# Sums of the weights for Strassen's scheme: formed in DRAM by transfers that add, in place of VectorE

## The chip, the cores and the metric

The kernel runs on one core of one Trainium2 chip. Time is device microseconds of one execution of the whole program; the lower, the better. Kernels are compared on the same chip in alternating rounds. Engines are named as the profile names them: PE is TensorE (PEld its weight loads), DVE is VectorE, ACT is ScalarE, POOL is GpSimd and SP is SyncE. ACT, POOL and SP each have a queue that issues transfers; a transfer is carried out by the core's 16 DMA engines.

## The reference

One layer of a streaming encoder on 512 tokens of 1024 channels, all in float32. What bears on the change are two of its products, the mixers' output projection and the MLP's down-projection.

```python
h = _rms_norm(x, norm_mix_pre[l])
(a_q, a_k, a_v, f_q, f_k, f_v, f_g, c_u, s_x, s_b, s_c) = jnp.split(h @ w_in[l], cuts, axis=-1)
...
proj = jnp.einsum('bsnc,ncd->bsnd', br, w_branch[l])
gates = jax.nn.sigmoid(h @ w_gate[l] + b_gate[l]).reshape(B, S, N_BRANCH, D)
mixed = jnp.sum(gates * proj, axis=2) @ w_out[l]          # (512, 1024) @ (1024, 1024)
x = x + _rms_norm(mixed, norm_mix_post[l])
...
u = _dwconv_causal(hf @ w_up[l], ffn_dw[l]) + ffn_dw_b[l]
u_g, u_v = jnp.split(u, 2, axis=-1)
yff = (jax.nn.silu(u_g) * u_v) @ w_down[l]                # (512, 2816) @ (2816, 1024)
x = x + _rms_norm(yff, norm_ffn_post[l])
```

`br` holds the four mixers' results: differential attention `ya`, forgetting attention `yf`, a convolution module and a short gated convolution. Between the mixers and the MLP stands a cross-attention into 256 memory tokens.

## The kernel before

*Products.* Each float32 product is made of three TensorE passes on a high and a low part in float32r (`mm3`): high by high, high by low, low by high. A weight tile of 128 rows by 1024 columns is loaded by SP into one of two raw tiles `wr` (L173), cast to the high part `wh` by ACT (L187), and the low part `wl` is the difference, by DVE (L188). There are four `wh` and four `wl`. `run_blocks` walks a list of jobs, most of them one such tile with 24 matmuls, and prepares three jobs ahead. A scheduler orders the instructions of each engine when the program is built; each engine then runs its own in that order.

*Background work.* The attention heads (`a_task`, `f_task`) and the convolution's normalization are generators that `bg.tick()` steps between jobs, so that their short matmuls, softmax steps and transposes lie between the jobs' long ones. POOL clears the unused halves of each head pair's q and k tile `qk` (L758), makes the reciprocal roots of the norms (`rstd_of`, L268 and L269), and for the forgetting attention the bias tiles `fbias` (L988 and L990, two buffers) that DVE adds to the scores (L994). POOL's queue also issues some loads, among them the rows `ck` (L958) that the biases are made of.

*Strassen's scheme.* The output projection (`mix_out_jobs`) and the down-projection (`down_jobs`) take the weights in pairs of 128-row blocks and each block in two halves of 512 columns. With the halves b11, b12 of a pair's first block and b21, b22 of its second, the seven products M1 to M7 need, beside the plain halves, four sums of halves. The activations' sums are made by `activation_sums`, on DVE for the output projection and on POOL for the down-projection (L564 to L567). The class `Sums` makes the weights' sums ahead of time: `load(q)` brings the two blocks of pair q to SBUF, `add(q)` makes four sums on DVE in place (L540 to L543), `store(q)` writes them to a DRAM tile, from which `load_parts` later brings what a product needs.

For w_out (four pairs, tiles `wide`, transfers on SP's queue) this is done among the first jobs of the mixers, around the gates of the short convolution; the tiles lie in the buffer that later holds the attention's v, so v is taken only in the last of its four jobs. For w_down (11 pairs, tiles `wp`, transfers on ACT's queue) it is done during the up-projection, one step a job: in the jobs of `up_jobs`, `add`, `store` and `load` take turns, each tied behind an instruction of that job by `issue_after`. The tiles `wp` share their four buffers with the tiles `dw` of the down-projection.

The order of the stages: convolution module and short convolution, their gates; v, then q and k of the differential attention with the convolution's gates between; v of the forgetting attention; its q and k with the gates of the first attention between; the last branch's gates (`last_branch_jobs`); output projection; cross-attention; up-projection; down-projection.

Of the kernel before, what the change touches and what calls it, by code (L numbers as in the profile page):

```python
# [24 lines left out]
P = 128  # L25
# [57 lines left out]
def hybrid_layer(ctx: ExitStack, tc: tile.TileContext, a: dict, out: bass.AP):  # L83
# [91 lines left out]

    def split_weights(raw, shape, low=V, order=same, shift=0):
# [10 lines left out]
        order(A.copy(hi, raw[:, :n]))  # L187
# [73 lines left out]
    def rstd_of(pool, parts, n=1):  # L261

        m = pool.tile([P, n], F32, tag="st_m", name="st_m", bufs=4)
        r = pool.tile([P, n], F32, tag="st_r", name="st_r", bufs=4)
        if len(parts) == 2:
            G.tensor_scalar(m, parts[0], parts[1], EPS, ALU.add, ALU.add)
        else:
            G.tensor_scalar(m, parts[0], EPS, None, ALU.add)  # L268
        G.tensor_tensor(r, m, nhalf[:, :n], ALU.pow)  # L269
        return r  # L270
# [254 lines left out]
    class Sums:  # L525


        def __init__(self, w, pairs, tile, queue, name):
            self.w, self.tile, self.queue, self.held = w, tile, queue, {}
            self.pairs, self.dram = pairs, dram.tile([pairs * P, 2 * D], F32, name=name)  # L530

        def load(self, q):
            if q < self.pairs:
                self.held[q] = [self.tile() for _ in range(2)]
                for i, x in enumerate(self.held[q]):
                    self.queue.dma_start(x, self.w[(2 * q + i) * P:(2 * q + i + 1) * P, :])

        def add(self, q):
            (b11, b12), (b21, b22) = ((x[:, :S], x[:, S:]) for x in self.held[q])
            V.tensor_tensor(b22, b22, b12, ALU.subtract)  # L540
            V.tensor_tensor(b12, b12, b11, ALU.subtract)
            V.tensor_tensor(b11, b22, b11, ALU.add)
            V.tensor_tensor(b21, b21, b11, ALU.subtract)  # L543

        def store(self, q):
            for i, x in enumerate(self.held.pop(q)):
                self.queue.dma_start(self.dram[q * P:(q + 1) * P, i * D:(i + 1) * D], x)

        def parts(self, phase, job, q):

            rows = [slice((2 * q + i) * P, (2 * q + i + 1) * P) for i in range(2)]
            t2, t1, n4, t3 = (self.dram[q * P:(q + 1) * P, i * S:(i + 1) * S] for i in range(4))
            return {(0, 0): (self.w[rows[0], :S], t2), (0, 1): (t1, t3), (1, 0): (self.w[rows[1], :],),
                    (1, 1): (n4,)}[phase, job]
# [194 lines left out]
    def qk_jobs(cq, ck, j, then):  # L749
# [5 lines left out]
        def body_q(hi, lo):  # L755
            qk = st["qk"] = m1p.tile([P, 6, S], F32R, tag="qk", name="qk", bufs=2)
            for c, r in enumerate(rows):
                G.memset(qk[rows[1 - c], 4 + c].bitcast(F32), 0.0)  # L758
# [192 lines left out]
    def f_task(p, qk, v):  # L951
# [10 lines left out]
        for step in range(6):  # L962
# [17 lines left out]
            if step < 4:  # L980
# [3 lines left out]
                for j in range(2):  # L984
# [5 lines left out]
                    G.affine_select(out=bias[:, w - P:w], in_=bias[:, w - P:w], pattern=[[-1, P]],  # L990
                                    compare_op=ALU.is_ge, fill=BIG, base=0, channel_multiplier=1)
# [64 lines left out]

    def kv_blocks(p):
        return qk_jobs(O_FQ, O_FK, p, lambda qk: bg.add(f_task(p, qk, vf), "f"))

    def mixer_jobs():  # L1060
# [4 lines left out]
        wide = m1p.tile([P, NT, D], F32, tag="v", name="wide")  # L1065
        free = iter([wide[:, i] for i in (0, 1, 2, 3) * 2])
        ns.out_sums = out_sums = Sums(w_out, NK // 2, lambda: next(free), SP, "out_sums")
        steps = {5: (out_sums.load, 0), 6: (out_sums.load, 1), 9: (out_sums.add, 0), 10: (out_sums.store, 0),
                 11: (out_sums.add, 1)}
        for i, job in enumerate(gate_blocks(3, "d")):  # L1070
            yield job
            if i in steps:
                yield then(lambda f=steps[i]: f[0](f[1]))
        yield then(lambda: y.pop("d"))
        vj = v_jobs(O_AV, va)
        yield then(lambda: (out_sums.store(1), out_sums.load(2), out_sums.load(3)) and None)
        for f, q in ((out_sums.add, 2), (out_sums.add, 3)):
            yield next(vj)
            yield then(lambda f=f, q=q: f(q))
            yield then(lambda q=q: out_sums.store(q))  # L1080
        yield from vj
        yield share(False)
        gc = gate_blocks(2, "c")
        for h, n in enumerate((0, 2, 4, 6)):
            yield from qk_jobs(O_AQ, O_AK, h, lambda qk, h=h: bg.add(a_task(h, qk, va), "a"))
            if n:
                yield then(lambda: bg.drain("conv"))
            for _ in range(n):
                yield next(gc)
        yield then(lambda: bg.drain("a"))  # L1090
        yield from vf_jobs(vf)
        yield from kv_blocks(0)
        ga = gate_blocks(0, "a")
        for p in range(1, 4):
            yield from kv_blocks(p)
            for _ in range(4):
# [96 lines left out]
    def last_branch_jobs():  # L1193
# [5 lines left out]
        yield from gf  # L1199
# [44 lines left out]
    def mix_out_jobs():  # L1244
# [50 lines left out]
        def middle(job):  # L1295
# [175 lines left out]
    def up_jobs():  # L1471
        st, held = {}, []

        def done(j, i, ps):
# [3 lines left out]
            st["first"] = A.activation(c[:, i], ps, AF.Identity, bias=pc("fb", ch), scale=pc("fdw2", ch)).ins  # L1478
            st["taps"] = taps(c[:, i], ps, lambda k: pc("fdw01", k * 44 + ch), 3).ins
# [252 lines left out]
```

## Time and profile before

| | |
|---|---|
| median of three runs | 1062.26 us (1062.02 to 1063.12) |
| profiled execution | 1062.36 us |
| its span, first to last instruction | 1060.5 us |
| mean granted clock of TensorE | 0.999 |
| moved by transfers in the span | 152.57 MB, 144 GB/s |

The span covers the first to the last instruction; the profiled execution's own time is 1.9 us longer. A group's row reads: line, engine, operation, output tile and inputs with shapes and count; then busy time and the mean of one in ns; then the idle time of the engine just before such instructions, with what ended it. Two rows of matmuls and the two of a weight tile's preparation:

```profile
L229 PE MATMUL ps_mm<-hth,wh 128*128 128x512 f32 (+1 forms) x616 | 231.5, 382 | 0.3 <-ACT hth L152 0.2
L229 PE MATMUL ps_mm<-htl,wh 128*128 128x512 f32 (+1 forms) x616 | 229.9, 380 | 0.0
...
L187 ACT CAST wh<-wr 128x1024 fp32r<-128x1024 f32 (+1 forms) x142 | 148.6, 1049 | 268.8 <-PE ps_mm L229 177.0
L188 DVE TENSOR_TENSOR wl<-wr,wh 128x1024 fp32r<-128x1024 f32 (+1 forms) x142 | 178.1, 1256 | 86.3 <-ACT wh L187 86.0
```

A matmul's own time here is from its start to its end through the pipeline; the next starts earlier, so rates are read from counts in a stretch of time.

### The profile page before, as it was taken

How to read it: one execution, taken by the hardware profiler on the slowest of the kernel's cores; microseconds unless marked ns; L12 is line 12 of the kernel's file. 1: busy time of each engine (PE TensorE's matmuls, PEld its weight loads, DVE VectorE, ACT ScalarE, POOL GpSimd, SP SyncE). 2: the span in 40 equal slices, each digit the busy share in tenths (PEclk: the TensorE clock that was granted, in tenths of full speed). 3: DMA queues.
4: the chain of work that ended last, by engine and by line, in shares of the span. 5: the costliest groups of instructions: out<-in, count | busy, mean ns of one | idle time of the engine just before them, and what ended most of it. 6: DMA issues, size and time to landing. Idle time of an engine off the chain costs nothing.

```text
span 1060.5 us, 14527 instructions
## 1 busy us (share of the span) xinstructions
PE 1051.5 (99%) x5363; PEld 894.0 (84%) x5363; DVE 797.1 (75%) x1261; ACT 497.6 (47%) x817; POOL 146.8 (14%) x233
## 2 busy tenths in 40 slices
PE   9999999999999999999999999999999999999997
PEld 8888888888888988888888899999888888888885
DVE  6899997567666358766575889786778787777796
ACT  5322222367565255655443565664333333445672
POOL 4000000000001015322110021031111211111001
PEclk9999999999999999999999999999999999999999
DMA  8854333322222252332344743226576776725672
GB/s 274 281 167 103 101 100 100 96 83 80 80 80 62 55 146 86 97 96 81 120 140 144 266 146 119 81 79 196 181 223 214 238 226 211 238 80 179 206 221 79
DMA packets 162107, 152.57 MB, mean 144 GB/s; under 512 B 5567, under 2 KB 135212, under 8 KB 162037
## 3 DMA queue, kind: packets, MB, share of 16 engines
q1 hardware_dynamic: 153139, 120.04, 37.7%
q10 hardware_dynamic: 6338, 23.08, 5.7%
q0 software_dynamic: 2560, 8.54, 2.7%
q8 instruction: 42, 0.69, 0.3%
q14 instruction: 28, 0.23, 0.1%
HBM read 133.79 MB, written 17.84 MB: 143 GB/s over the span
## 4 chain that ended last, share of the span: by engine, by line
PE 99%; DVE 0%; ACT 0%; issue 0%; POOLq 0%; DVEq 0%; POOL 0%; ACTq 0%
PE ps_mm L229 53%; PE ps_av L229 30%; PE ps_sc L229 7%; PE ps_tr L229 4%; PE ps_tr L233 3%; PE ps_mm L440 1%; PE ps_av L440 1%; PE ps_mm L382 0%; PE ps_sc L387 0%; DVE o L1632 0%; PE ps_tr L424 0%; DVE wr L1647 0%; DVE o L1623 0%; ACT ge L1029 0%; DVE o L1647 0%
## 5 line engine op out<-in xcount | busy, mean ns | idle before, releaser
L187 ACT CAST wh<-wr 128x1024 fp32r<-128x1024 f32 (+1 forms) x142 | 148.6, 1049 | 268.8 <-PE ps_mm L229 177.0
L188 DVE TENSOR_TENSOR wl<-wr,wh 128x1024 fp32r<-128x1024 f32 (+1 forms) x142 | 178.1, 1256 | 86.3 <-ACT wh L187 86.0
L229 PE MATMUL ps_mm<-hth,wh 128*128 128x512 f32 (+1 forms) x616 | 231.5, 382 | 0.3 <-ACT hth L152 0.2
L229 PE MATMUL ps_mm<-htl,wh 128*128 128x512 f32 (+1 forms) x616 | 229.9, 380 | 0.0
L229 PE MATMUL ps_mm<-hth,wl 128*128 128x512 f32 (+1 forms) x616 | 229.8, 379 | 0.0
L229 PEld LDWEIGHTS ps_mm<-hth,wh 128*128 128x128 f32 x616 | 114.2, 188 | 21.7 <-ACT hth L152 0.8
L229 PEld LDWEIGHTS ps_mm<-hth,wl 128*128 128x128 f32 x616 | 113.9, 188 | 21.2
L229 PEld LDWEIGHTS ps_mm<-htl,wh 128*128 128x128 f32 x616 | 114.1, 188 | 20.4 <-DVE htl L153 0.2
L229 PE MATMUL ps_av<-hth,wh 128*128 128x512 f32 (+1 forms) x328 | 122.7, 374 | 0.0
L229 PE MATMUL ps_av<-hth,wl 128*128 128x512 f32 (+1 forms) x328 | 122.5, 373 | 0.0
L229 PE MATMUL ps_av<-htl,wh 128*128 128x512 f32 (+1 forms) x328 | 122.4, 373 | 0.0
L662 DVE SCALAR_TENSOR_TENSOR y<-y,par,y 128x482 f32<-128x482 f32 (+29 forms) x120 | 82.8, 728 | 0.2
L229 PEld LDWEIGHTS ps_av<-htl,wh 128*128 128x128 f32 x328 | 61.7, 188 | 10.9
L229 PEld LDWEIGHTS ps_av<-hth,wl 128*128 128x128 f32 x328 | 61.7, 188 | 10.8
L229 PEld LDWEIGHTS ps_av<-hth,wh 128*128 128x128 f32 x328 | 61.5, 188 | 10.8
L1534 DVE TENSOR_TENSOR wl<-dw,wh 128x1024 fp32r<-128x1024 f32 x32 | 40.2, 1261 | 12.2 <-ACT wh L1533 12.1
L1533 ACT CAST wh<-dw 128x1024 fp32r<-128x1024 f32 x32 | 33.5, 1052 | 22.5 <-PE ps_tr L229 8.3
L988 POOL TENSOR_SCALAR fbias<-ck,cq 128x128 f32<-128x128 f32 (+3 forms) x32 | 27.5, 865 | 68.8 <-DVE st L994 61.9
L1482 ACT ACTIVATE th<-c 128x512 f32<-128x512 f32 x22 | 13.9, 632 | 48.5 <-DVE c L592 48.5
L152 ACT CAST pth<-ps_tr 128x512 fp32r<-128x512 f32 (+3 forms) x56 | 23.4, 448 | 21.6 <-PE ps_tr L233 21.5
L592 DVE SCALAR_TENSOR_TENSOR c<-ps_mm,par,c 128x510 f32<-128x510 f32 (+1 forms) x44 | 32.7, 744 | 0.7
L153 DVE TENSOR_TENSOR ptl<-ps_tr,pth 128x512 fp32r<-128x512 f32 (+3 forms) x56 | 27.9, 512 | 5.6 <-ACT pth L152 5.4
(466 smaller groups left out, 2099.2 us busy)
## 6 DMA issues: line engine op xcount, KB each, us to landing
wr<-in_w_up SPq DMA_DIRECT2D x44, 512.0 KB
wr<-in_w_in SPq DMA_DIRECT2D x38, 512.0 KB
wr<-in_w_gate SPq DMA_DIRECT2D x32, 512.0 KB
wp<-in_w_down ACTq DMA_DIRECT2D x22, 512.0 KB
sums<-wp ACTq DMA_DIRECT2D x22, 512.0 KB
dw<-sums SPq DMA_DIRECT2D x44, 256.0 KB
wr<-in_w_branch SPq DMA_DIRECT2D x16, 512.0 KB
wide<-in_w_out SPq DMA_DIRECT2D x12, 512.0 KB
```

Of the source, the lines that this page charges most:

```text
L152: A.copy(hi, ps)
L153: V.tensor_tensor(lo, ps, hi.bitcast(F32), ALU.subtract)
L187: order(A.copy(hi, raw[:, :n]))
L188: low.tensor_tensor(lo, raw[:, :n], hi.bitcast(F32), ALU.subtract)
L229: PE.matmul(ps, lhs, rhs, start=start, stop=stop)
L233: PE.transpose(ps, x, ident[:n, :n])
L440: keep(PE.matmul(banks[c][:, :S // 2], w[p == 1][:, k, c * P:(c + 1) * P], ht[p == 2][:, i * 4 + k, :S // 2], start=(i, p, k) == (0, 0, 0) ...
L592: ins = V.scalar_tensor_tensor(dst[:, s:], src[:, :S - s], w(k), dst[:, s:], ALU.mult, ALU.add)
L662: ins = V.scalar_tensor_tensor(dst[:, s:], src[:, :S - s], pc("conv_dw", k * 4 + j), dst[:, s:], ALU.mult, ALU.add)
L988: G.tensor_scalar(bias[:, :w], ck[j][:, :w], -1.0, cq[:, qt, head:head + 1], ALU.mult, ALU.add)
L1533: A.copy(hi, x)
L1534: V.tensor_tensor(lo, x, hi.bitcast(F32), ALU.subtract)
```

## The change

The sums of the weights are no longer made in SBUF. For each chunk of four pairs (three in w_down's last) there are four DRAM tiles p1 to p4 of 512 columns. ACT's queue copies a half into each, from DRAM to DRAM; then POOL's queue issues four transfers that add:

- p1 = b11 + b12
- p3 = b12 + b22
- p2 = b22 + p1
- p4 = b21 + p2

Before, the four were b11 + b22 - b12, b12 - b11, b22 - b12 and b21 - b11 - b22 + b12. With adding alone the second half of each block counts with the other sign, so one activation sum, the last activation sum and the combinations with M5 and M7 turn a sign; each stays one instruction of the same kind on the same operands.

The 32 steps (8 for a chunk, one chunk of w_out and three of w_down) are handed out one at a time by `sums_step`, which `paced` puts after each job from v of the differential attention to the last branch; between the steps of w_down an empty one is put, so that they come every second job. A step is tied on its engine behind the latest entry of a log: `cast_log` holds ACT's casts of weights, `pool_log` POOL's roots, clears and bias selections. Each tile of the sums is then read by `load_parts` as before.

```diff
-        def load(self, q):
-            if q < self.pairs:
-                self.held[q] = [self.tile() for _ in range(2)]
-                for i, x in enumerate(self.held[q]):
-                    self.queue.dma_start(x, self.w[(2 * q + i) * P:(2 * q + i + 1) * P, :])
-
-        def add(self, q):
-            (b11, b12), (b21, b22) = ((x[:, :S], x[:, S:]) for x in self.held[q])
-            V.tensor_tensor(b22, b22, b12, ALU.subtract)
-            V.tensor_tensor(b12, b12, b11, ALU.subtract)
-            V.tensor_tensor(b11, b22, b11, ALU.add)
-            V.tensor_tensor(b21, b21, b11, ALU.subtract)
...
+        def steps(self):
+
+            for i, sums in enumerate(self.sums):
+                n = sums[0].shape[0] // P
+                w = self.w[2 * i * self.chunk * P:][:2 * n * P]
+                b11, b12, b21, b22 = (w.rearrange("(q i p) c -> i p q c", i=2, p=P)[r][:, :, c * S:(c + 1) * S]
+                                      for r in range(2) for c in range(2))
+                p1, p2, p3, p4 = (t.rearrange("(q p) c -> p q c", p=P) for t in sums)
+
+                for dst, src in (p1, b11), (p3, b12), (p2, b22), (p4, b21):
+                    yield cast_log, lambda dst=dst, src=src: A.dma_start(dst, src)
+                for dst, src in (p1, b12), (p3, b22), (p2, p1), (p4, p2):
+                    yield pool_log, lambda dst=dst, src=src: G.dma_start(dst, src, accum_op=ALU.add)
...
-        eng.tensor_tensor(x[:, 2], x[:, 1], z[:, 1], ALU.add)
+        eng.tensor_tensor(x[:, 2], x[:, 1], z[:, 1], ALU.subtract)
         eng.tensor_tensor(x[:, 3], x[:, 0], x[:, 1], ALU.subtract)
         eng.tensor_tensor(x[:, 1], x[:, 2], x[:, 0], ALU.subtract)
-        eng.tensor_tensor(z[:, 2], z[:, 0], x[:, 1], ALU.subtract)
+        eng.tensor_tensor(z[:, 2], z[:, 0], x[:, 1], ALU.add)
...
-                if kb == 3:
+                if kb == 0:
                     v = m1p.tile([P, 2, NT, BR], F32R, tag="v", name="v")
...
+    def sums_step():
+        step = next(ns.steps, None)
+        if step:
+            log, f = step
+            with tc.issue_after(log[-1]):
+                f()
+
+    def paced(jobs):
+
+        for job in jobs:
+            yield job
+            yield then(sums_step)
...
+        ns.out_sums, ns.sums = Sums(w_out, NK // 2, 4, "os"), Sums(w_down, NF // 2, 4, "ds")
+        ns.steps = iter([f for f in ns.out_sums.steps()] + [f for g in ns.sums.steps() for f in (None, g)])
+        yield from paced(v_jobs(O_AV, va))
         yield share(False)
-        gc = gate_blocks(2, "c")
+        gc = paced(gate_blocks(2, "c"))
...
-                V.tensor_tensor(u[:, t], u[:, t], banks["M5"][t], ALU.add)
+                V.tensor_tensor(u[:, t], banks["M5"][t], u[:, t], ALU.subtract)
             for t in range(2):
-                V.tensor_tensor(place(2 + t, 1), u[:, t], banks["M7"][t], ALU.add)
+                V.tensor_tensor(place(2 + t, 1), u[:, t], banks["M7"][t], ALU.subtract)
...
-                    q = n // 3 - 2
-                    if 0 <= q < NF // 2:
-                        with tc.issue_after(st["taps" if n % 3 == 0 else "first"]):
-                            (ns.sums.add, ns.sums.store, ns.sums.load)[n % 3](q + 2 * (n % 3 == 2))
...
-                    ns.sums = Sums(w_down, NF // 2, lambda: ns.fp.tile([P, D], F32, tag="dw", name="wp", bufs=4), A,
-                                   "sums")
-                    ns.sums.load(0)
-                    ns.sums.load(1)
```

More of the change, by code (lines that the diff above doesn't have):

```diff
@@ L538, in add, with __init__ @@
-        def add(self, q):
-            (b11, b12), (b21, b22) = ((x[:, :S], x[:, S:]) for x in self.held[q])
[L540 to L547, printed above, removed]
+        def __init__(self, w, pairs, chunk, name):
+            self.w, self.chunk, self.sums = w, chunk, []
+            for q in range(0, pairs, chunk):
+                n = min(chunk, pairs - q)
+                self.sums.append([dram.tile([n * P, S], F32, name=f"{name}{q}_{i}") for i in range(4)])
@@ L549, in parts @@
         def parts(self, phase, job, q):
             rows = [slice((2 * q + i) * P, (2 * q + i + 1) * P) for i in range(2)]
-            t2, t1, n4, t3 = (self.dram[q * P:(q + 1) * P, i * S:(i + 1) * S] for i in range(4))
-            return {(0, 0): (self.w[rows[0], :S], t2), (0, 1): (t1, t3), (1, 0): (self.w[rows[1], :],),
-                    (1, 1): (n4,)}[phase, job]
+            k = q % self.chunk
+            p1, p2, p3, p4 = (t[k * P:(k + 1) * P, :] for t in self.sums[q // self.chunk])
@@ L556, in load_parts @@
+            return {(0, 0): (self.w[rows[0], :S], p2), (0, 1): (p1, p3), (1, 0): (self.w[rows[1], :],),
+                    (1, 1): (p4,)}[phase, job]
     def load_parts(raw, parts):
```

58 lines of the change are left out of this document (22 added, 36 removed).

## The prediction, made before the changed kernel had run

> **What bounds the kernel now.** I read the page first: busy time by engine, then the chain of work that ended last.
>
> ```profile
> PE 1051.5 (99%) x5363; PEld 894.0 (84%) x5363; DVE 797.1 (75%) x1261; ACT 497.6 (47%) x817; POOL 146.8 (14%) x233
> ...
> PE 99%; DVE 0%; ACT 0%; issue 0%; POOLq 0%; DVEq 0%; POOL 0%; ACTq 0%
> ```
>
> TensorE is busy for 1051.5 of 1060.5 us, and the chain runs through it alone. So the question is where the 9.0 us without TensorE lie, and whether its busy time hides waits. The second view is the busy time in stretches of 20 us (columns: length, PE, PEld, DVE, ACT, POOL, each with its count of instructions, then granted clock, DMA share, GB/s).
>
> ```profile
> 0.00:20.00 20.00, 18.44 (x115) 15.67 (x116) 13.85 (x22) 11.28 (x20) 11.80 (x23) 1.00 0.80 257
> ...
> 20.00:40.00 20.00, 19.98 (x154) 18.79 (x153) 17.40 (x32) 8.55 (x12) 0.00 (x0) 1.00 0.82 266
> ...
> 60.00:80.00 20.00, 20.00 (x90) 16.57 (x89) 20.00 (x30) 5.77 (x8) 0.00 (x0) 1.00 0.46 132
> ...
> 400.00:420.00 20.00, 19.88 (x106) 16.46 (x105) 15.56 (x45) 12.21 (x32) 9.73 (x20) 1.00 0.36 106
> ...
> 700.00:720.00 20.00, 19.76 (x146) 18.36 (x146) 14.70 (x17) 10.81 (x21) 5.78 (x9) 1.00 0.44 132
> ...
> 860.00:880.00 20.00, 20.00 (x90) 16.57 (x89) 15.82 (x19) 7.76 (x10) 4.53 (x4) 1.00 0.72 233
> ...
> 1040.00:1060.00 20.00, 13.42 (x60) 10.78 (x58) 13.60 (x21) 4.35 (x12) 4.35 (x8) 0.95 0.28 105
> ```
>
> 1.56 us are missing in the first stretch and 6.58 us in the last, plus the 0.5 us after it: 8.64 us of start and end that the change does not touch. All the rest of the span has some 0.4 us of idle TensorE, almost all of it in 20:40, 400:420 and 700:720. Hidden waits would show as a pitch that changes. It does not: 60:80 has 20.00 us of VectorE work and 860:880 has 15.82, with DMA shares of 0.46 and 0.72, and both hold 90 matmuls. The chain in order of time gives the pitch:
>
> ```profile
> 763.55 5.44 PE ps_mm L229 x24
> ```
>
> 5.44/24 = 0.227 us for a matmul of 512 columns; one product of a weight tile (a job, below) is 24 of them.
>
> **The change part by part.** *Removed from VectorE:* four sums a pair, 4 pairs of w_out at 25 to 62 us and 11 of w_down from 720 us on.
>
> ```profile
> L542 DVE TENSOR_TENSOR wp<-wp 128x512 f32<-128x512 f32 x11 | 9.7, 880 | 0.2
> L543 DVE TENSOR_TENSOR wp<-wp 128x512 f32<-128x512 f32 x11 | 8.6, 782 | 0.0
> L541 DVE TENSOR_TENSOR wp<-wp 128x512 f32<-128x512 f32 x11 | 7.6, 689 | 0.2
> L540 DVE TENSOR_TENSOR wp<-wp 128x512 f32<-128x512 f32 x11 | 7.5, 682 | 0.0
> ...
> L540 DVE TENSOR_TENSOR wide<-wide 128x512 f32<-128x512 f32 x4 | 2.8, 688 | 5.1 <-DMA wide<-in_w_out 5.1
> ```
>
> 9.7 + 8.6 + 7.6 + 7.5 = 33.4 us in the MLP, and about 4 x 2.8 = 11 us near the start with 5.1 us of waiting for the rows of w_out: some 45 us of work and 5 of waiting. It lies beside matmuls at full pitch, so it is worth 0 to the end; at most it returns the 0.4 us of idle time. I take 0.
>
> *Removed transfers:* the rows loaded and the sums stored.
>
> ```profile
> wp<-in_w_down ACTq DMA_DIRECT2D x22, 512.0 KB
> sums<-wp ACTq DMA_DIRECT2D x22, 512.0 KB
> ...
> wide<-in_w_out SPq DMA_DIRECT2D x12, 512.0 KB
> ...
> out_sums<-wide SPq DMA_DIRECT2D x8, 512.0 KB
> ```
>
> For the sums, 22 + 22 loads and stores go from ACT's queue and 8 + 8 from SP's (four of the 12 rows named wide<-in_w_out are later loads of the products and stay). They freed no TensorE time where they ran, by the equal pitch above: 0.
>
> *Added:* 16 copies from DRAM to DRAM on ACT's queue and 16 adding transfers on POOL's, 1 MB each (12 of each kind; the last chunk of three pairs has 0.75 MB). No row of the trace adds in a transfer, so its time is bounded.
>
> ```profile
> q1 hardware_dynamic: 153139, 120.04, 37.7%
> ...
> m_t<-in_mem POOLq DMA_DIRECT2D x2, 512.0 KB, 5.0
> ...
> crows<-e POOLq DMA_DIRECT2D x1, 16.0 KB, 2.2
> ```
>
> From below: 120.04 MB took 37.7% of 16 engines for 1060.5 us, 400 us of all sixteen, or 3.3 us a MB. An add has to read the old value too, so twice that, 6.7 us, and the 2.2 us that even a small transfer of POOL's queue needs: 8.9 us. From above, from that queue's own 512 KB: (5.0 - 2.2) x 2 for a MB, x 2 for two reads, + 2.2 = 13.4 us. I take 13, near the end that comes from the same queue; the adding itself could make it longer, and that is the first rival. [...]
>
> *Where POOL's queue stands still.* In a chunk the third add reads the first's result and the fourth the third's, and the wait stands on POOL, whose later work queues behind it. For w_down the steps come every second job. SP's loads, one a job, give a job's length in this stage:
>
> ```profile
> 226.60 0.37 SPq L173 DMA_DIRECT2D wr<-in_w_in  x1
> ...
> 308.79 0.37 SPq L173 DMA_DIRECT2D wr<-in_w_branch  x1
> ```
>
> There are twelve intervals between these two: 82.2/12 = 6.85 us, so 13.7 us for two jobs. A 13 us add is done when the next is due: no wait. For w_out the steps come every job; its fourth add waits 13 - 6.85 = 6 us. What stands behind it on POOL in the built order is the clearing of the zero halves of a later head's q and k tile, some four jobs away: 0. Without that cover it would be 6 us once. Behind w_down's adds stand the biases of the forgetting attention:
>
> ```profile
> DVE e L994 <- POOL fbias L990: 3.1, 2, 2.4
> ...
> POOL fbias L988 <- DVE st L994: 61.9, 15, 16.7
> ```
>
> (engine, line, released by: us, times, longest). In 32 softmax steps VectorE waited for a bias twice, 3.1 us in all; POOL itself waited for its buffers 61.9 us in 15 times, 4 us on average. A POOL delay under 4 us is mostly swallowed there, a longer one reaches the scores, the transposes and so TensorE.
>
> *Issuing:*
>
> ```profile
> L958 POOL DMA_DIRECT2D ck<-crows x8 | 4.7, 584 | 1.8 <-DMA crows<-e 1.8
> ...
> 753.36 0.34 ACTq L547 DMA_DIRECT2D sums<-wp  x1
> ```
>
> 16 x 0.584 = 9 us more on POOL, one at a time, each under the 4 us above; ACT issues 16 instead of 44, 28 x 0.34 = 9.5 us less. From below 0, from above the four to six that stand between biases, 6 x 0.584 = 3.5 us. I take 0.4 us of it on the path, close to 0 because a bias was last in only 2 of 32 steps.
>
> *DMA engines.* The adds and copies run in about 160:560.
>
> ```profile
> 160.00:560.00 400.00, 399.88 (x2070) 340.02 (x2069) 259.80 (x543) 204.78 (x390) 64.25 (x115) 1.00 0.32 94
> ...
> L187 ACT CAST wh<-wr 128x1024 fp32r<-128x1024 f32 (+1 forms) x62 | 64.8, 1048 | 101.3 <-PE ps_mm L229 74.8 <-PE ps_av L229 21.7 <-issue 2.4
> ```
>
> 15 MB copied and 15 MB added cost 15 x 3.3 + 15 x 6.7 = 150 us of all engines, +0.38 on a share of 0.32: 0.70, below one. The second row is the cast of the loaded weights in the same stretch: of 101.3 us in which ACT waited before it, 96.5 were for TensorE to free the tile, so the loads are early. A tile is cast about three jobs before its use, 3 x 5.44 = 16 us; a load behind one whole add is 13 us late and still no stall: 0. Without this cover, each add would cost up to 13 us.
>
> *Moved or of equal cost:* turned signs keep their instruction counts and sizes; a v tile is taken at the first of four jobs instead of the last; the first sums of the down-projection are loaded before the up-projection's later weights, as their tiles no longer hold w_down's rows. In the built order the two programs have the same number of matmuls of each shape; TensorE's order differs in the attention stages alone and is the same from the last branch on. 0, with the 0.4 us of idle time found either way for other waits at the new places.
>
> Sum: profiled run 1062.36 (span 1060.5 and 1.9 around it) + 0 + 0.4 = 1062.8; that run lies 0.1 above the median of 1062.26, so **1062.7 us**.
>
> **The rivals.**
>
> 1. *Slower: POOL stands behind an add that is longer than two jobs.* It decides from 13.7 + 4 = 18 us an add. For it: no row bounds the adding itself, and its packets share engines with the loads. Against: 8.9 to 13.4 us from rows. At 22 us each chunk's fourth add waits 8 us on POOL; less 4 us of slack that is 4 us, for two chunks amid attention work 8 us: 1070.7. At 30 us it is 2 x 12 = 24: 1087. [...]
> 2. *Slower by order:* new places of scores, transposes and value products on TensorE meet results that are not there. One missed wait is priced like the two late biases above, 3.1/2 = 1.6 us; two of them: 1062.7 + 3.2 = 1065.9. Against: 0.4 us of idle time is all that the old order of the same kind left.
> 3. *Faster:* VectorE's relief pulls in waits that the busy records of the attention stages hide. 160:560 holds 399.88 us of busy time; 1% of it, ten times the idle time found, would be 4 us: 1058.7. Against: the pitch in 60:80, where VectorE was full, is that of the stretches where it was not.
> 4. *The sums stay on VectorE in some form:* excluded, its built order is 64 rows shorter and has no sum of weights left.
>
> **How the numbers follow.** About 0.2%, 2.1 us, is what a measurement of this kernel can tell from no change. The forecast of no change 0.58, its own range 1060.3 to 1064.4; rival 1 0.20; rival 2 0.12; rival 3 0.10. Faster 0.10, same 0.58, slower 0.32. The range reaches to rival 3's smaller half, 1060, and on the other side past rival 2 to rival 1 at about 21 us an add: 1069. What is left out is some 0.05 below and 0.10 above.
>
> **What would show it.** Right: 90 matmuls per 20 us in 60:160 and 740:940 as now, VectorE some 45 us less busy, idle TensorE outside start and end still under 1 us, adds that land within 9 to 14 us, no POOL wait on an add over 4 us but w_out's fourth. Rival 1: POOL waits for adds over 8 us, then VectorE waiting for fbias beyond 3.1 us, then TensorE idle in 380:540. Rival 2: TensorE gaps in 200:540 without a POOL wait before them. Wrong altogether: a pitch other than 0.227 us, or ACT waiting for wr loads in 160:560.

## The result, and the profile after

The changed kernel takes 1081.41 us (median of four runs, 1080.03 to 1081.66); the kernel before takes 1062.69 beside it. The ratio is 1.0164, with a 95% interval of 1.0133 to 1.0195: 1.6% slower, where 1062.7 us and no change were forecast, and well above the range. The profiled execution has a span of 1079.4 us, 18.9 more than before. The page of the kernel after, its busy line and its chain by line:

```profile
PE 1058.1 (98%) x5363; PEld 897.1 (83%) x5363; DVE 758.9 (70%) x1201; ACT 497.7 (46%) x817; POOL 161.3 (15%) x249
...
PE 89%; DMA 5%; DVE 3%; ACT 1%; issue 1%; POOL 0%; POOLq 0%; DVEq 0%; ACTq 0%
PE ps_mm L233 47%; PE ps_av L233 27%; PE ps_sc L233 7%; PE ps_tr L233 4%; DMA wr<-in_w_gate 3%; PE ps_tr L237 3%; DMA wr<-in_w_in 2%; DVE wl L192 1%; ACT wh L189 1%; PE ps_mm L444 1%; PE ps_av L444 1%; PE ps_mm L386 0%; DVE qk L767 0%; PE ps_sc L391 0%; DVE o L1629 0%
```

The chain was TensorE alone; now 5% of it are loads of weights (`wr`), and the cast and the difference that follow a load have entered with them. VectorE is busy for 38 us less, and nothing came of it. Stretches of the kernel after (columns as in the prediction; the DMA share adds up the packets' times, so it passes 1 where packets overlap, as with 1.09 in 200:220):

```profile
180.00:200.00 20.00, 20.00 (x94) 16.70 (x93) 8.31 (x12) 3.74 (x4) 2.90 (x5) 1.00 0.55 148
200.00:220.00 20.00, 16.40 (x76) 13.17 (x75) 8.45 (x11) 10.07 (x16) 3.47 (x4) 0.95 1.09 289
220.00:240.00 20.00, 16.07 (x61) 12.70 (x60) 8.02 (x11) 8.07 (x13) 1.24 (x1) 0.88 0.96 208
380.00:400.00 20.00, 17.46 (x94) 14.77 (x93) 10.90 (x24) 9.92 (x16) 0.00 (x0) 0.98 0.93 291
400.00:420.00 20.00, 20.00 (x91) 16.49 (x90) 11.02 (x26) 11.58 (x22) 6.87 (x15) 0.94 0.55 159
440.00:460.00 20.00, 18.95 (x96) 15.39 (x95) 11.19 (x28) 9.81 (x21) 7.80 (x13) 1.00 0.72 163
460.00:480.00 20.00, 19.12 (x103) 15.97 (x102) 15.47 (x38) 11.36 (x25) 8.36 (x13) 1.00 0.89 188
860.00:880.00 20.00, 20.00 (x90) 16.57 (x89) 12.88 (x16) 6.44 (x8) 2.94 (x4) 1.00 0.37 106
...
160.00:560.00 400.00, 388.01 (x1982) 327.93 (x1981) 240.11 (x516) 195.53 (x377) 78.35 (x123) 0.99 0.59 155
```

The missing busy time is 3.60 + 3.93 + 2.54 + 1.05 + 0.88 = 12.0 us; 160:560 as a whole lacks the same 12.0. The granted clock is below 1 in four rows, and (0.05 + 0.12 + 0.02 + 0.06) x 20 = 5.0 us of full clock are lost there. That is 17.0 of the 18.9 us; the other 1.9 were not traced. The MLP's 860:880 still holds 90 matmuls. What ends the idle time in 200:240, from the chain in order of time:

```profile
196.50 1.06 ACT wh L189
197.56 0.02 issue
197.58 1.24 DVE wl L192
198.82 0.02 issue
198.84 14.03 DMA wr<-in_w_in
...
212.96 1.05 ACT wh L189
214.02 0.02 issue
214.04 1.24 DVE wl L192
215.28 0.02 issue
215.29 14.18 DMA wr<-in_w_gate
...
234.06 7.31 PE ps_mm L233 x24
```

When `wl` is made its raw tile is free, and the tile's next load starts; it takes 14.03 and 14.18 us (in the kernel before, loads of this stage had moved their last packet 3.2 to 3.6 us after their issue), the cast and the difference follow, and only then does the load behind it in the same tile start. Two such turns in a row are 33 us, and TensorE runs dry in both. The last row is a product of 24 matmuls that lasts 7.31 us instead of 5.44: part of it runs at half clock (the record of the granted clock has 0.5 for 3.41 us from 235.19 on). The waits of ACT, POOL and DVE of the same kernel that bear on it (us, times, longest), and its adding transfers (the last column is from issue to landing):

```profile
ACT wh L189 <- DMA wr<-in_w_gate: 14.9, 3, 6.9
ACT wh L189 <- DMA wr<-in_w_in: 11.2, 2, 8.4
```

```profile
POOL os L550 <- DMA os<-in_w_out: 24.5, 2, 13.0
```

```profile
DVE e L999 <- POOL fbias L994: 2.1, 2, 1.3
```

```profile
ds<-in_w_down POOLq DMA_DIRECT2D x4, 1024.0 KB, 9.7
ds<-ds POOLq DMA_DIRECT2D x4, 1024.0 KB, 10.7
...
os<-in_w_out POOLq DMA_DIRECT2D x2, 1024.0 KB, 12.7
os<-os POOLq DMA_DIRECT2D x2, 1024.0 KB, 10.5
```

An add of 1 MB takes 9.7 to 12.7 us, inside the 8.9 to 13.4 of the prediction. So the adds are as long as thought; what is wrong is what they do to others.

### The profile page after: what moved, and what is told of

It is laid out like the page before. It is cut to its first block, busy times and chain, and to the rows that moved or that the text cites. A ratio compares the mean times of both kernels' runs of the same rounds, so it can differ in the third digit from the quotient of the medians.

```text
span 1079.4 us, 14386 instructions
## 1 busy us (share of the span) xinstructions
PE 1058.1 (98%) x5363; PEld 897.1 (83%) x5363; DVE 758.9 (70%) x1201; ACT 497.7 (46%) x817; POOL 161.3 (15%) x249
## 4 chain that ended last, share of the span: by engine, by line
PE 89%; DMA 5%; DVE 3%; ACT 1%; issue 1%; POOL 0%; POOLq 0%; DVEq 0%; ACTq 0%
PE ps_mm L233 47%; PE ps_av L233 27%; PE ps_sc L233 7%; PE ps_tr L233 4%; DMA wr<-in_w_gate 3%; PE ps_tr L237 3%; DMA wr<-in_w_in 2%; DVE wl L192 1%; ACT wh L189 1%; PE ps_mm L444 1%; PE ps_av L444 1%; PE ps_mm L386 0%; DVE qk L767 0%; PE ps_sc L391 0%; DVE o L1629 0%
## 5 line engine op out<-in xcount | busy, mean ns | idle before, releaser
L666 DVE SCALAR_TENSOR_TENSOR y<-y,par,y 128x506 f32<-128x506 f32 (+29 forms) x120 | 83.0, 730 | 0.3
L1488 ACT ACTIVATE th<-c 128x512 f32<-128x512 f32 x22 | 13.9, 631 | 43.4 <-DVE c L596 43.4
L152 ACT CAST pth<-ps_tr 128x512 fp32r<-128x512 f32 (+3 forms) x56 | 23.5, 448 | 17.1 <-PE ps_tr L237 16.9
```

Source lines behind the costliest of these rows:

```text
L152: A.copy(hi, ps)
L666: ins = V.scalar_tensor_tensor(dst[:, s:], src[:, :S - s], pc("conv_dw", k * 4 + j), dst[:, s:], ALU.mult, ALU.add)
```

## The experiments

Ratios are to the kernel before, timed on the same chip in the same batch, since its median was 1062.4 to 1066.0 us from batch to batch, and its executions within one batch spread over 3.7 to 7.3 us.

**First question: the DMA engines or POOL's queue.** E says that copies and adds together fill the DMA engines, so that loads of weights come late. Q says that POOL stands at its adds, and what is queued behind them comes late.

*No add waits for an add* (the second pair of adds reads the weights, not the first pair's sums):

```diff
-                for dst, src in (p1, b12), (p3, b22), (p2, p1), (p4, p2):
+                for dst, src in (p1, b12), (p3, b22), (p2, b11), (p4, b12):
```

> The third and fourth add of a chunk take a half of the weights in place of an earlier sum (the third b11, the fourth b12), so no add waits for another add; bytes, adds and places in the order stay, and the sums are other numbers. Theory E (the DMA engines: copies and adds fill them, the loads of wr land late): same demand on the engines, so 1078 to 1084 us, and loads of 10 us and more around 200 to 240 us. Theory Q (POOL's queue stands at adds that wait for adds, and the clears, norms and biases behind them come late): those waits are gone, 1064 to 1068 us.

Measured: 1079.32 us, ratio 1.0148 (1.0126 to 1.017). Nearly all of the loss is left, so POOL's waits for its own sums are not it.

*Copies alone* (the 16 adds left out):

```diff
-                for dst, src in (p1, b12), (p3, b22), (p2, p1), (p4, p2):
-                    yield pool_log, lambda dst=dst, src=src: G.dma_start(dst, src, accum_op=ALU.add)
+                for _ in range(4):
+                    yield pool_log, lambda: None
```

> The 16 adds are left out, the 16 copies stay; the sums are plain halves. Theory E: the demand in 200 to 240 us falls from 1.0 of the engines to about 0.6, and the loss there goes; the loss at 380 to 400 us, where only copies ran beside the loads (2.5 us idle and 1.7 us of half clock), stays: 1065 to 1069 us. Theory Q: POOL waits for no transfer any more, nothing is lost: 1062 to 1064 us.

Measured: 1068.17 us, 1.0042 (1.0023 to 1.006).

*The same transfers on POOL, but they overwrite instead of adding:*

```diff
-                    yield pool_log, lambda dst=dst, src=src: G.dma_start(dst, src, accum_op=ALU.add)
+                    yield pool_log, lambda dst=dst, src=src: G.dma_start(dst, src)
```

> POOL's 16 transfers write over their target and do not add; waits, order and bytes named stay, but a packet needs one read (84 ns expected in place of 178 ns). Theory E: 3 us less of all engines per transfer, the 40 us around 220 us need some 0.75 of the engines: 1065 to 1072 us. Theory Q: each wait for a transfer gets shorter only by those 3 us of 10 to 13, so two thirds of the loss stay: 1074 to 1078 us.

Measured: 1067.63 us, 1.0049 (1.003 to 1.0067). POOL still waits in this run, as its rows show:

```profile
POOL os L550 <- DMA os<-in_w_out: 11.6, 1, 11.6
POOL ds L550 <- DMA ds<-ds: 9.8, 1, 9.8
...
POOL os L550 <- DMA os<-os: 7.2, 1, 7.2
```

So the same queue with the same waits costs no more than the copies do. Q falls; by the ratios the adding itself costs some 12 us, the copies some 5. VectorE waited 5.0 us for a bias in this run, but the run of copies alone, in which POOL issues no transfer of the sums, has that wait too:

```profile
DVE e L999 <- POOL fbias L994: 5.1, 1, 5.1
```

```profile
391.47 6.76 DMA ck<-crows
```

The second row is from that run's chain in order of time: the rows `ck`, of which the bias is made, took 6.8 us while copies ran beside them (3.8 in the kernel before), and TensorE's longest gap there, 1.9 us at 398, ends behind this bias. So a part of what the copies cost is a late load of another kind, not of a weight tile.

*w_out's sums on VectorE again* (at their old place, with the new signs), w_down's in DRAM:

```diff
+        ns.sums = Sums(w_down, NF // 2, 4, "ds")
+        ns.steps = iter([None] * 4 + [f for g in ns.sums.steps() for f in (None, g)])
         yield from vj
```

> The sums of w_out are again made on VectorE at their old place (with the new signs), those of w_down stay transfers that add at their places. Theory E: the idle time and half clock of 200 to 240 us, 7.5 + 3.4 us, go and the rest stays: 1069 to 1072 us. Theory Q: w_out's 36 of 53 us of POOL waits for transfers go, about two thirds of the loss: 1067 to 1071 us. This run places the loss more than it tells the two apart.

Measured: 1069.78 us, 1.0066 (1.0041 to 1.0092): 200 to 240 us is full, and what is left is lost at 385 and around 450. All four agree with E; this last time lies in Q's range too.

**Second question: closeness or volume.** B says that a load is late only where transfers come close together, V that every MB costs the same.

*w_down's sums on VectorE again, w_out's in DRAM* (the mirror of the last):

```diff
-        ns.out_sums, ns.sums = Sums(w_out, NK // 2, 4, "os"), Sums(w_down, NF // 2, 4, "ds")
-        ns.steps = iter([f for f in ns.out_sums.steps()] + [f for g in ns.sums.steps() for f in (None, g)])
+        ns.out_sums = Sums(w_out, NK // 2, 4, "os")
+        ns.steps = iter([f for f in ns.out_sums.steps()])
```

> The kernel after, but w_down's sums are made on VectorE in the up-projection again (with the new signs, rows loaded and sums stored by ACT's queue); only w_out's chunk is copied and added in DRAM. Two theories of how the filled DMA engines cost time. B (bunching): a load is late only where copies and adds come close together, or where no tile is prepared ahead; w_out's chunk alone then keeps all it costs at 200 to 240 us in the kernel after (7.5 us without a matmul and two spells of half clock of 1.7 us each), and 380 to 400 is full: 1062.4 + 7.5 + 3.4 = 1073.3, between 1071 and 1075. V (volume): each MB costs the same wherever it is moved; w_out is 4 of 15 pairs, 4/15 of 18.7 us = 5.0: 1067.4, between 1066 and 1069.

Measured: 1074.24 us, 1.0088 (1.0065 to 1.0111). By ratio that is 9 us for 4 of 15 pairs, where V has 5: against V.

*w_out's steps at half the pace*, from the short convolution's gates on:

```diff
-        yield from gate_blocks(3, "d")
+        yield from paced(gate_blocks(3, "d"))
...
-        ns.steps = iter([f for f in ns.out_sums.steps()] + [f for g in ns.sums.steps() for f in (None, g)])
+        ns.steps = iter([f for g in ns.out_sums.steps() for f in (None, g)] + [None] * 4
+                        + [f for g in ns.sums.steps() for f in (None, g)])
```

> The kernel after, with w_out's eight transfers handed out every second job, from the short convolution's gates on, instead of every job; w_down's stay at their places. Same transfers, same sizes. B: the stretch 200 to 240 is full again and only the loss at 380 to 400 and at 450 to 465 is left, as where w_out's sums were put back on VectorE (1069.8): between 1067 and 1072. V: the same bytes, so 1079 to 1083.

Measured: 1074.61 us, 1.0085 (1.0058 to 1.0111): neither. The pace at which steps are handed out is not that at which POOL runs them; its timeline:

```profile
182.07 0.51 POOL L272 TENSOR_SCALAR st_m<-bn 128x1 f32<-128x1 f32 x2 [5.83 <-DVE bn L682]
182.66 1.08 POOL L273 TENSOR_TENSOR st_r<-st_m,nhalf 128x1 f32<-128x1 f32 x2
183.69 2.66 POOL L550 DMA_DIRECT2D os<-in_w_out  x2
192.90 1.24 POOL L550 DMA_DIRECT2D os<-os  x1 [6.54 <-DMA os<-in_w_out]
```

The copies went out from 149.6 us on, but the adds stood behind the roots of the convolution's norm, which waited for DVE's statistics (`bn`), and then came out together.

*The same bytes in 60 copies and 60 adds of 0.25 MB*, one of each a job:

```diff
+        ns.out_sums, ns.sums = Sums(w_out, NK // 2, 1, "os"), Sums(w_down, NF // 2, 1, "ds")
+        steps = [*ns.out_sums.steps(), *ns.sums.steps()]
+        copies = [f for f in steps if f[0] is cast_log] + [None] * 5
+        adds = [None] * 5 + [f for f in steps if f[0] is pool_log]
+        ns.steps = iter(zip(copies, adds))
```

> The kernel after, with the same bytes copied and added, but in 60 copies and 60 adds of 0.25 MB (a pair at a time), one copy and one add a job from the short convolution's gates on. B: no stretch of 20 us has a DMA share above 0.85, loads are at most one small add late (some 3 us), the clock is full: 1061.5 to 1065. V: the same bytes, 1079 to 1083, more if the 120 issues of 0.6 us weigh on POOL and ACT.

Measured: 1075.03 us, 1.0093 (1.0071 to 1.0115). B's range was missed for the same reason (four adds leave POOL within 4 us at 183.8, and a load is waited for 13.0 us), and a second spell is lost at 389.

*The same with a pause of six jobs around v of the forgetting attention*, and adds two jobs behind their copies instead of five:

```diff
-        copies = [f for f in steps if f[0] is cast_log] + [None] * 5
-        adds = [None] * 5 + [f for f in steps if f[0] is pool_log]
-        ns.steps = iter(zip(copies, adds))
+        copies = [f for f in steps if f[0] is cast_log] + [None] * 2
+        adds = [None] * 2 + [f for f in steps if f[0] is pool_log]
+        both = list(zip(copies, adds))
+        ns.steps = iter(both[:36] + [None] * 6 + both[36:])
```

> As the kernel with 0.25 MB transfers, one copy and one add a job, but with six jobs without any around v of the forgetting attention, where the four held tiles leave no load ahead. B: what is left of waiting at 380 to 400 in the kernel without the pause goes: 1061 to 1064, and at most equal to it. V: 1079 to 1083, as without the pause.

Measured: 1065.45 us beside 1065.82, ratio 1.0001 (0.999 to 1.0013). This is the whole change, all bytes copied and added, and it costs nothing that the timing can tell (the interval is 1.1 us below to 1.4 us above). The pause and the shorter lag of the adds came together, so which of them counted is not shown. Its stretches:

```profile
180.00:200.00 20.00, 20.00 (x94) 16.62 (x93) 8.58 (x12) 3.74 (x4) 6.51 (x10) 1.00 0.87 192
200.00:220.00 20.00, 20.00 (x97) 16.61 (x96) 11.71 (x15) 13.91 (x20) 5.91 (x8) 1.00 0.91 219
```

V falls. But TensorE is full here beside DMA shares of 0.87 and 0.91, so the share does not tell where time is lost. One gap is left, at 373 us; the waits of TensorE have it:

```profile
PE ps_mm L233 <- DVE v L153: 1.4, 1, 1.4
```

**Third question: the place.** R says that only jobs of 5.44 us, in the v stages and before them, use tiles up faster than late loads bring them; P that closeness costs the same anywhere.

*w_out's chunk ten jobs later* (w_down's sums on VectorE):

```diff
-        ns.steps = iter([f for f in ns.out_sums.steps()])
+        ns.steps = iter([None] * 10 + [f for f in ns.out_sums.steps()])
```

> w_down's sums on VectorE as in the run that cost 1074.2, and w_out's four copies and four adds again one a job, 1 MB each, but starting ten jobs later, behind v of the differential attention, among jobs that attention work stretches to some 6.85 us. R (rate): beside back-to-back adds a load takes 14 us, with two raw tiles in flight that is a tile every 7 us; jobs of 5.44 us (v's, and those before it) use tiles up faster and lose their lead, jobs of 6.85 us do not. So the loss goes though the same eight transfers run as close together: ratio to before 0.999 to 1.003. P (place does not matter, only closeness): the loss stays, ratio 1.007 to 1.011 as without the shift.

Measured: 1073.62 us, 1.0079 (1.0059 to 1.0099). The loss moved along with the adds. A stretch of it, and a link of its chain in order of time:

```profile
300.00:320.00 20.00, 13.88 (x66) 11.09 (x65) 9.09 (x17) 8.53 (x17) 3.52 (x4) 0.96 1.00 207
```

```profile
296.37 17.70 DMA wr<-in_w_gate
```

*16 and 16 transfers of 1 MB as in the change, but none in the v stages:*

```diff
+        w_down_steps = [*ns.sums.steps()]
+        ns.steps = iter([None] * 6 + [*ns.out_sums.steps()] + w_down_steps[:6] + [None] * 8
+                        + [f for g in w_down_steps[6:] for f in ([None, g] if g[0] is pool_log else [g])])
```

> The kernel after with its 16 copies and 16 adds of 1 MB, but none handed out in v of the differential attention and the two jobs behind it, nor from four jobs before v of the forgetting attention to four behind it; in between they come closer than in the kernel after (every job, and no empty step before a copy). R: the losses at 200 to 240 and at 380 to 400 both go, what was lost at 450 to 465 (2 us) stays or grows a little: ratio to before 1.000 to 1.005. P: at least as slow as the kernel after, ratio 1.015 to 1.022.

Measured: 1074.19 us, 1.0086 (1.0063 to 1.011), between the two, with a gap of 5.05 us at 290 behind a load of 17.1.

*w_down's chunks alone, earlier and with a pause around v:*

```diff
-        ns.steps = iter([None] * 4 + [f for g in ns.sums.steps() for f in (None, g)])
+        paced_steps = [f for g in ns.sums.steps() for f in (None, g)]
+        ns.steps = iter(paced_steps[:20] + [None] * 6 + paced_steps[20:])
```

> w_out's sums on VectorE at the old place, w_down's copies and adds in DRAM every second job as in the run that cost 1069.8 (ratio 1.0066), but started four jobs earlier and with six jobs without any around v of the forgetting attention. R: the 3.3 us gap at 385 and the half clock behind it go, the small gaps at 445 to 454 stay: ratio 1.000 to 1.003. P: nothing changes, ratio 1.005 to 1.009.

Measured: 1074.2 us, 1.009 (1.0067 to 1.0112). The gap at 385 shrank to 1.45 us and a new one of 4.43 came at 314, where POOL had released two adds at once (294.46). R falls: the place decides little, P is right in that.

**Fourth question: why a load takes 14 to 18 us.** The packets of the transfers, from the trace's records: those that start in each 3 us, with the size and the median time of one (load: SP's queue, add: POOL's, copy: ACT's).

```
                          load             add                copy
before, 240-244 us        915 of 512 B, 27 ns
w_out later, 303-306      247 of 512 B, 41   249 of 2 KB, 176
w_out later, 306-309      258 of 512 B, 41   241 of 2 KB, 176
w_out later, 258-261       52 of 512 B, 27                   483 of 2 KB, 84
```

(The first row is of 4 us.) A copying packet of 2 KB takes 84 ns, an adding one 176 to 178, and while add and load run together there are as many packets of the one as of the other. The loads of w_in and w_gate have 1024 packets, 64 for each engine; 64 x (176 + 41) ns = 13.9 us, against 64 x 27 = 1.7 us of their own. The two overlap a little: from 303 to 309 us each queue starts 16 packets, as many as there are engines, every 194 ns, so 64 turns are 12.4 us. The load they belong to lasted 17.70 us; its first packet came 3.7 us after its issue (1.0 in the kernel before) and its packets ran for some 13. The turns fit those 13; why the first packet came late is not shown. For the loads of 14 us in the kernel after, the nearness to 13.9 is chance: the one of 14.03 had its first packet after 3.8 us, took turns with an add and a copy up to 205 us (274 ns for the three) and then mostly with a copy alone (104 to 106 ns for the two). K says that this is it: packets take turns, and a load pays for its number of packets by the other's size. G says that bytes, or engine time, decide.

*All transfers in packets of 512 bytes* (each as four of 128 columns):

```diff
-                    yield cast_log, lambda dst=dst, src=src: A.dma_start(dst, src)
+                    yield cast_log, lambda dst=dst, src=src: [A.dma_start(dst[:, :, c:c + P], src[:, :, c:c + P])
+                                                                   for c in range(0, S, P)]
...
-                    yield pool_log, lambda dst=dst, src=src: G.dma_start(dst, src, accum_op=ALU.add)
+                    yield pool_log, lambda dst=dst, src=src: [G.dma_start(dst[:, :, c:c + P], src[:, :, c:c + P], accum_op=ALU.add)
+                                                                   for c in range(0, S, P)]
```

> The kernel after, with each copy and each add of 1 MB issued as four of 128 columns: the same bytes at the same places, in packets of 512 bytes instead of 2 KB. K (packets take turns): while an add and a load run together the trace has as many packets of the one as of the other (303 to 312 us in the run with w_out's chunk later: 737 of 2 KB at 176 ns, 755 of 512 bytes at 41 ns), so a load of 1024 packets, 64 an engine, lasts 64 x 0.217 = 13.9 us whatever its bytes. An adding packet of 512 bytes should take about 2 x 27 = 54 ns, so a load takes 64 x 0.095 = 6.1 us beside an add, some 8 beside an add and a copy; its lead covers that, and most of the loss goes: ratio to before 1.000 to 1.006. G (bytes, or engine time): the DMA engines have the same bytes to move and add, in more packets, so the same share or more, and the loss stays: ratio 1.014 to 1.025. Either way the 64 + 64 issues cost POOL about 48 x 0.8 us more, which no theory so far puts on the path.

Measured: 1082.5 us, 1.0167 (1.014 to 1.0194). That is G's range. It does not decide, as a second thing changed: ACT's waits for loads of w_gate fell to 3.6 us at the longest, but ACT, which casts the weights, now stood at its own copies. Its timeline (length of the issues, and their count at the end of the row), where four issues took 2.63 us at first and two took 6.46 later:

```profile
196.09 2.63 ACTq L548 DMA_DIRECT2D os<-in_w_out  x4
...
204.80 6.46 ACTq L548 DMA_DIRECT2D os<-in_w_out  x2
...
211.44 2.68 ACTq L548 DMA_DIRECT2D os<-in_w_out  x1
```

*The adds alone in packets of 512 bytes*, in the run with w_out's chunk later, where the copies have landed before the adds start (the second half of the diff above):

> The kernel with w_down's sums on VectorE and w_out's chunk ten jobs later (ratio 1.0079, a gap of 4.9 us at 313 behind a load of 17.7 us, and 6.8 us of half clock), with its four copies as they were and only its four adds cut into four of 128 columns each, packets of 512 bytes. The copies have landed before the adds start there, and ACT issues what it did, so nothing but the adding packets beside the loads is changed. K (packets take turns): 64 x (0.064 + 0.041) = 6.7 us a load beside an add instead of 13.9; no gap at 313, no half clock: ratio 0.999 to 1.003. G (bytes, or engine time): four adds take 4 x 2048 x 4 x 64 ns / 16 = 131 us of engine time over all sixteen divided by 4 MB, 33 us instead of 23, the share is as full for longer: ratio 1.006 to 1.012.

Measured: 1064.9 us beside 1065.38, ratio 0.9999 (0.9984 to 1.0013). The loss is gone. The stretches at the same place:

```profile
300.00:320.00 20.00, 20.00 (x101) 16.76 (x100) 12.12 (x22) 11.92 (x23) 10.53 (x10) 1.00 1.30 200
320.00:340.00 20.00, 20.00 (x104) 16.91 (x103) 13.96 (x38) 11.34 (x25) 6.90 (x8) 1.00 0.91 175
```

The DMA share is 1.30 instead of 1.00, and TensorE has no gap there. Of the two w_gate loads beside the adds, the longer moved its last packet 9.9 us after its issue, and a turn of the two queues had become 81 ns; in the run before, the longer one needed 17.3 us and a turn 194 ns. The same place, the same bytes, the same queue: K is shown for adds beside loads, at this place, and G falls.

*The same cut with w_out's chunk at the place of the change*, beside copies:

> The same cut of the adds alone, with w_out's chunk at the place of the kernel after (ratio 1.0088 with adds of 2 KB packets), where copies of 2 KB packets run beside them. K: a load beside both lasts 64 x (0.064 + 0.098 + 0.041) = 13 us instead of 20, and 6.7 beside an add alone: about half the loss goes, ratio 1.001 to 1.006. G: ratio 1.008 to 1.013.

Measured: 1072.27 us, 1.0064 (1.0045 to 1.0084) instead of 1.0088, just outside K's range, and the two intervals overlap. Its longest load takes 15.08 us, the next 11.37.

*The same cut in all four chunks*, in the run that hands out nothing in v:

> The whole change again, w_out's and w_down's chunks in DRAM, paced as in the kernel that hands out nothing in v (ratio 1.0086: gaps of 5.05 us at 290, 0.8 at 320, 1.4 at 381 and 1.4 at 424, half clock of 3.4 us at 295), with only the adds cut into packets of 512 bytes. K (packets take turns): the gap at 290 and the half clock go, as adds alone stood beside that load; what copies do beside loads stays: ratio 1.000 to 1.004. G (bytes, or engine time): the adds take 1.44 times the engine time they took, ratio 1.008 to 1.015.

Measured: 1071.02 us, 1.0059 (1.0038 to 1.008) instead of 1.0086: outside K's range, with intervals that overlap. The gap at 290 is gone, as expected; two smaller ones came at 313 and 315, with 3.4 us of half clock behind them. They come from where copies run too, behind a load that landed 14.3 us after its issue:

```profile
280.00:300.00 20.00, 20.00 (x102) 16.91 (x102) 12.21 (x32) 9.29 (x24) 8.59 (x8) 1.00 1.24 263
300.00:320.00 20.00, 17.27 (x78) 13.80 (x77) 12.01 (x22) 11.60 (x21) 3.54 (x4) 0.94 1.08 236
```

In its records of 306 to 309 us there are 302 packets of loads, 291 of adds and 302 of copies: three queues take turns, and 64 x (41 + 64 + 84) ns = 12.1 us a load (10.3 by the 161 ns in which each queue starts 16 packets). The expectation had taken the copies' part of a turn as small. That the copies cause what is left of the loss in these two runs is read from the records and was not tried by itself.

## Why the prediction was wrong

- *Bound.* TensorE sets the end, and 8.6 us of start and end stay: right.
- *Sums removed from VectorE, transfers removed: 0.* Right. The sums' 33.4 + 11.0 us are gone as said (the busy time, in which instructions that overlap count once, falls by 38), the MLP kept its 90 matmuls, and the whole change spread out and paused has ratio 1.0001. Rival 3, faster, has nothing in it that a run shows.
- *The adding transfer: 8.9 to 13.4 us, taken as 13.* Right, 9.7 to 12.7. That a second read doubles the time was the author's estimate, and no run shows the read apart from the adding. What the runs show are the packets: 178 ns for an adding one of 2 KB against 84 for a copying one, a factor of 2.1; at 512 bytes it is 64 against 27, a factor of 2.4.
- *POOL's queue.* The price, near 0, was right, the picture was not. Adds do not run every second job; they are tied to POOL's own order, which is not tied to TensorE's, so they wait behind other work of POOL and then follow one another. POOL waited up to 13.0 us before an add (4 were named as the sign of being right), but VectorE's wait for biases stayed at 2.1 us. Rival 1 had the first half of its signs and not the second; without the chain of adds at most some 2 of 19 us went (the intervals of the two ratios overlap).
- *Issuing.* POOL is 14.5 us busier instead of 9, and overwriting transfers with the same issues kept only the copies' loss: nothing seen on the path, where 0.4 was taken.
- *Rival 2, order.* It has one of the waits that it priced at 1.6 us each. The two runs with ratios 1.0001 and 0.9999 both keep a gap of 1.4 to 1.5 us at 373 us, among the jobs of v of the forgetting attention, where the kernel before has none; the load that ends it lasts 3.9 to 4.0 us, and no copy or add runs beside it. What took that load's lead is not shown. The gaps of the kernel after that were traced, from 200 to 240 us, end behind late loads, so this rival is at most a small part of the 18.9 us.
- *"DMA engines": this is the step that failed.* It said: a share of 0.70, below one; a load behind one whole add 13 us late; 16 us of cover; 0. The runs showed 12.0 us without a matmul and 5.0 of half clock in its place. The share over 160:560 came out lower, 0.59, and it was the wrong quantity twice over. First, an average over 400 us hides 1.09 and 0.96 in 200:240, as the adds run when POOL is free. Second, the runs show time lost at shares of 0.72 and none at 1.30: what a load beside an add paid was its number of packets times a turn with the add's (64 x 194 ns = 12.4 of some 13 us, with w_out's chunk later). That one load lasted 14.0 us, near the 13 taken, is luck, as it did not stand behind one add but took turns with several transfers; one such load the cover of 16 us would have borne. But w_out's four copies and four adds run from 190 to 238 us with two pauses of some 2 us (512 packets of each MB at 84 and at 178 ns, over 16 engines: 4 x 8.4 = 34 us of all engines), a raw tile's load waits for the cast of the one before, and the late loads add up: two in a row use up the 16 us. The prediction had the price, "without this cover, each add would cost up to 13 us", and gave it neither a place in the sum nor a rival with a chance. The rows that would have warned were there: 153139 packets for 120.04 MB on the loads' queue, under 1 KB each, beside new transfers in rows of 2 KB; and adds of 13 us handed out every 6.85.
- *Not in the prediction at all:* the clock. 5.0 of the 18.9 us are TensorE at half clock after its gaps. "A pitch other than 0.227 us, or ACT waiting for wr loads in 160:560" was named as the sign of being wrong altogether, and both came.

## What to carry to other kernels

When transfers are added beside loads that must be on time, compare the sizes of their packets before their bytes: here a load in many small packets took turns with the other queue's packets one for one, and the large ones set its time (with w_out's chunk later, 17.3 us beside adds of 2 KB, 9.9 beside adds of 512 bytes). Take the share of the DMA engines from the stretch where the new transfers really run (here 1.09 in 200:220 against 0.59 over 160:560), which here followed the order of the queue that issues them and not the pace at which the program hands them out. And price a short wait of TensorE with the half clock that can follow it: here 5.0 us beside 12.0 without a matmul.

## What the runs showed of the hardware

*Turns.* Beside an add a load's packets come one for one: 247 and 249, 258 and 241 in the rows above, 302, 291 and 302 with three queues. With w_out's chunk later, from 303 to 309 us, the load's and the add's queue each start 16 packets, as many as there are engines, every 194 ns, a little under the 176 + 41 ns of one packet of each.

*Size and adding.* A copying packet takes 27 ns at 512 bytes (all transfers in small packets) and 84 at 2 KB (the kernel after); an adding one 64 and 176 to 178. Cut to 512 bytes, adds thus need 4 x 64 / 178 = 1.44 times the engine time, and with w_out's chunk later the kernel was faster for it, ratio 0.9999 instead of 1.0079.

*Clock.* In the kernel after, the records of the granted clock have, between the start and the end of the program, three spells of 0.5, each 3.413 us long, that start at 218.122, 235.189 and 399.029: 5 and 48 times 3.413 us apart. Each follows a gap of TensorE of 2.3 to 4 us within three microseconds. In other runs a gap of 4.89 us was followed by 6.83 us of half clock (w_out's chunk later) and one of 1.79 by 3.41 (overwriting transfers), but one of 1.44 by none (0.25 MB with a pause); of two of 2.53 and 2.07 us in the run at half pace only the second was. So gaps of 1.8 to 4.9 us were followed by half clock in these cases, while gaps of 1.44 and of 2.53 us were not; what decides between the two is not shown.
